# Buffers, loads and places of work moved in a one-layer encoder kernel with attention and a delta-rule recurrence

## The chip, the cores and the metric

The kernel runs on one core of a Trainium2 chip. The metric is the time of one execution in microseconds of device time (us); lower is better. TensorE is the matrix engine (PE in the profile; PEld is its loading of weights), VectorE is DVE, ScalarE is ACT, GpSimd is POOL, and SyncE (SP) issues most transfers. TensorE's clock has two levels, 1.2 and 2.4 GHz; the profile gives the granted clock as a share of 2.4 GHz, so 0.50 is the low level.

## The reference

One layer, on 2048 tokens of width 1024 in float32. The input is normed and projected; half of the columns go to a neighbourhood attention (8 heads of 64, a window of 8 rows by 16 columns on a grid 64 tokens wide), the other half to a gated delta rule that runs over the sequence forwards and backwards (4 heads of 128). Both halves are gated, put side by side, projected out and added to the input.

```python
h = _rmsnorm(x, norm_w)
proj = h @ w_in                                   # 1024 -> 4112 columns
attn = _neighbourhood_attention(aq, ak, av, rpb) * silu(az)
dq, dk, dv = split(silu(conv5(cat([dq, dk, dv]))))          # centred, depthwise
o_f = _gated_delta_chunked(dq, dk, dv, g_f, beta_f)         # S <- decay*S + k^T v_new
o_b = flip(_gated_delta_chunked(flip(dq), flip(dk), flip(dv), flip(g_b), flip(beta_b)))
delta = _rmsnorm(o_f + o_b) * silu(dz)
return x + cat([attn, delta]) @ w_out
```

## The kernel before, in words

A float32 product is made of three products of rounded parts (high by high, high by low, low by high). The work has four stages, one behind the other on TensorE.

The first two stages are the two halves of the projection (`conv_group` for the columns that are convolved, `token_group` for the others; half 1 begins with `conv_group(1, 0)`). Beside them run tasks of a small planner in the code: `tick` moves a clock of the planner's own, `spawn` and each `yield` give a task a due time on it, and a task's instructions are written into the program when its due time has passed. TensorE keeps the program's order there (the class `InOrder` chains each product to the one before). A `token_group` without gates ticks sixteen times 1.42, so 22.72 in all; 24 of its products are 2.84 of the planner's us. The tasks that the change touches are these:

- `turn` transposes a convolved tile of 128 columns, some ticks after its convolution; the tuple `lag` holds how many (half 1 has twelve tiles, `tl` 0 to 11).
- `prepare(half)` solves small triangular systems: `blocks` on VectorE for one direction, then for the other (`ready[d]` is set when a direction's blocks are done, and `solved` with the second). Then joins put the blocks together: `join` issues its loads (E, W and T), yields 14.2, and makes the products `pa`, `pb`, `pc` and `pd`, each 2.84 behind the one before, with a copy on ScalarE between them. In half 0 `both` runs the joins of both directions in step, four times; in half 1 three lanes share ten joins. When the last lane is done it opens the pools for attention's inputs (`open_values`).
- `drain` runs tasks without any projection work beside them.

The third stage is attention (`attend`): 64 units (head pair p, group of rows g, group of columns cg), each with scores on TensorE, a reduction with bias on VectorE, an exponential on ScalarE, a scaling on VectorE, transposes, a copy and the values. The units' instructions are chained to each other on each engine. The recurrence's `step` for both directions is traced behind every seventh unit, the first behind unit 7; its instructions are not chained, and the compiler's scheduler, which lays each engine's order by its own estimate of the times, may put them earlier or later. The four first output weight parts are split (`early_wout`) behind units 52 to 58.

The fourth stage is the output: `late_wout` splits the other four parts of the output weight, and then, for s = 8 to 15, two steps of the recurrence and two `finish` (norm, gate, transposes, the output product `py` and the sum with x).

SBUF is handed out in pools as two stacks, one from either end; a new tile that lies where an old one lay waits until the old one's last use is over. Buffers of attention lie where buffers of the projection lay, and buffers of the output stage lie where attention's lay.

```python
at = {NA_S0 + NA_S1 * i: i for i in range(9)}      # behind units 7, 14, ... 63
...
for s in range(8, 16):
    if s < 15:
        self.step(0, s + 1, False)
        self.step(1, 14 - s, False)
    self.finish(s)
    self.finish(15 - s)
```

Of the kernel before, what the change touches and what calls it, by code (L numbers as in the profile page):

```python
# [70 lines left out]
class Trunk:  # L71
# [198 lines left out]
    def taps(self, half, tl, cb, os):  # L270
# [24 lines left out]
        lag = (21, 29, 36, 33, 30, 27) if half == 0 else (28, 28, 28, 28, 30, 30, 30, 30, 34, 34, 34, 34)  # L295
# [310 lines left out]
    def both(self, pj, c0, c1, sj):  # L606

        W = [pj.tile([128, 8, 128], F32, name=f"wb{d}") for d in range(2)]
        T = [pj.tile([128, 8, 64], F32, name=f"tb{d}") for d in range(2)]
        for t in W + T:  # L610
            self.G.memset(t, 0.0)
        while len(self.ready) < 2:
            yield 1.4
        for c in range(c0, c1, 2):
            e = min(c + 2, c1)
            sinks = [], []
            yield from self.together([self.join(d, c, e, pj, d, W[d], T[d], sinks[d]) for d in range(2)], sinks)
            self.joined += 2
        sj.close()

    def lane(self, i, pj, jobs, sj, c0):

        held = None
        while jobs:
            d = jobs[0][0]
            if d != held:
                W = pj.tile([128, 8, 128], F32, tag=f"wn{i}", name=f"wn{i}{jobs[0][1]}{d}")
                T = pj.tile([128, 8, 64], F32, tag=f"wt{i}", name=f"wt{i}{jobs[0][1]}{d}")
                self.G.memset(W, 0.0)
# [7 lines left out]
            yield from self.together([self.join(d, c, c1, pj, i, W, T, sink)], [sink])  # L637
# [47 lines left out]
    def join(self, d, c, c1, pj, lane, W, T, sink):  # L685
# [13 lines left out]
        yield 14.2  # L699
# [75 lines left out]
    def load_gates(self, p, g):  # L775
        z = self.z[p, g] = self.ns.tile([128, 512], F32, tag="z", name=f"z{p}{g}")
# [8 lines left out]
    def feed(self, p, g):  # L785

        if g == 0:
            if p == 0:
                self.load_bias(0, 1)
                self.load_gates(0, 0)  # L790
            self.load_bias(p, 2)
        elif g == 1 and p < 3:
            self.load_heads(p + 1)
# [28 lines left out]
    def scores(self, p, g, cg):  # L822

        V, A, PE = self.V, self.A, self.PE
        if cg == 0:
            self.feed(p, g)
            mn = self.ns.tile([128, 8], F32, tag="mn", name=f"mn{p}{g}")
            sm = self.ns.tile([128, 8], F32, tag="sm", name=f"sm{p}{g}")
# [55 lines left out]
    def open_recurrence(self, st):  # L884
        P = lambda *a, **k: self.pool(st, *a, **k)
        self.lp, self.op, self.sp, self.rf, self.fx = P("rl", 3), P("ro", 16), P("rs", 2), P("rf", 2), P("rx", 2)
        self.woh, self.wol = [], []
# [13 lines left out]
    def split_wout(self, k, h, l):  # L901
        r = self.fx.tile([128, 1024], F32, tag="x", name=f"wo{k}")
        self.dma(r, self.io["w_out"][:, k])
        self.A.activation(h, r, AF.Copy)
        (self.G, self.V)[k % 2].tensor_tensor(out=l, in0=r, in1=h.bitcast(F32), op=ALU.subtract)
# [3 lines left out]
    def early_wout(self, k):  # L909

        if k < 2:
            t = self.nh[0].tile([128, 2048], F32R, tag="qk"[k], name=f"wo{k}p")
            self.split_wout(k, t[:, :1024], t[:, 1024:])
        else:
            self.split_wout(k, *(self.nv[0].tile([128, 1024], F32R, tag=f"v{2 * k - 4 + i}", name=f"wo{k}p{i}") for i in range(2)))
# [5 lines left out]
    def step(self, d, c, first):  # L921
# [12 lines left out]
        G.tensor_tensor(out=kt, in0=kt, in1=self.eK[:, u0 : u0 + 4].unsqueeze(2).to_broadcast([128, 4, 128]), op=ALU.mult)  # L934
# [3 lines left out]
        for h in range(4):  # L938
            PE.matmul(pk[:, h], kq[:, h, 0], s0[:, h], start=True, stop=True)  # L939
# [38 lines left out]
    def finish(self, c):  # L978
# [16 lines left out]
        na = fp.tile([128, 4, 128], F32, tag="na", name=f"na{c}")  # L995
        dma(na, self.na_d.rearrange("(p k) n -> k p n", k=128)[:, :, cs])
        x = self.fx.tile([128, 1024], F32, tag="x", name=f"x{c}")
        dma(x, self.io["x"][cs])
# [4 lines left out]
        for j, t in enumerate((na, o)):  # L1003
# [7 lines left out]
            V.tensor_tensor(out=lo[:, sl], in0=pt, in1=hi[:, sl].bitcast(F32), op=ALU.subtract)  # L1011
        last = c in (0, 15)
# [17 lines left out]
    def run(self):  # L1030
        with ExitStack() as st:
# [84 lines left out]
            self.late_wout()  # L1116
            for s in range(8, 16):
                if s < 15:
                    self.step(0, s + 1, False)
                    self.step(1, 14 - s, False)  # L1120
                self.finish(s)
# [67 lines left out]
```

## Time and profile before

| what | value |
|---|---|
| time, median of 3 runs | 1439.64 us (1437.33 to 1440.28) |
| the profiled execution: its own time | 1437.78 us |
| the profiled execution: span from first to last instruction | 1436.0 us |
| TensorE busy | 1371.1 us, 95% of the span |
| VectorE, ScalarE, GpSimd busy | 904.1, 664.1, 174.0 us |
| mean granted clock of TensorE | 0.985 |

The span has some 1.8 us around it in the profiled execution's time. The stages stand in the span about like this: half 0 of the projection to 428 us, half 1 to 893, attention to 1166, output to the end. A busy share near 100% of TensorE in a stretch means that TensorE's own work sets the length of that stretch.

### The profile page before, as it was taken

Reading aid. Unit: us, or ns where it says so; the run is one execution under the profiler, and the core shown is the slowest. Engines: PE = TensorE matmul, PEld = TensorE weight load, DVE = VectorE, ACT = ScalarE, POOL = GpSimd, SP = SyncE. Lnnn points to the kernel's source line nnn. Section 1 sums busy time; section 2 is a strip of 40 time slices with the busy share of each in tenths; the row PEclk is TensorE's granted clock in tenths of the full one; section 3 lists DMA queues with packets and bytes.
Section 4 is the critical chain, followed back from the end, with each engine's and each line's share of the span. In section 5 each row is a group of like instructions: output and inputs, shape, how many; then the busy total and the mean of one; then the engine's idle time right before and its main releaser. Section 6 shows DMA issues by size and latency. Waiting matters only on the chain.

```text
span 1436.0 us, 28123 instructions
## 1 busy us (share of the span) xinstructions
PE 1371.1 (95%) x10570; PEld 1181.9 (82%) x10570; DVE 904.1 (63%) x2211; ACT 664.1 (46%) x1630; POOL 174.0 (12%) x206
## 2 busy tenths in 40 slices
PE   7999999999799998999999999899999989999998
PEld 6788988999696886887999888677777767888887
DVE  5689645667434657796887210667768758766773
ACT  6475235733254555464434443656667642221220
POOL 0001102121000021011110110010001012111110
PEclk9999999999899999999999999999999999999999
DMA  9263346774465443678656843999887466765632
GB/s 340 75 237 106 85 132 208 263 218 115 94 197 191 158 133 136 191 240 283 165 126 186 211 135 118 316 313 250 249 224 259 146 186 195 219 199 188 198 103 73
DMA packets 274621, 267.91 MB, mean 187 GB/s; under 512 B 92982, under 2 KB 218038, under 8 KB 273462
## 3 DMA queue, kind: packets, MB, share of 16 engines
q1 hardware_dynamic: 229276, 211.39, 50.0%
q10 hardware_dynamic: 45210, 54.73, 11.2%
q8 instruction: 84, 1.38, 0.4%
q14 instruction: 51, 0.42, 0.1%
HBM read 186.70 MB, written 79.36 MB: 185 GB/s over the span
## 4 chain that ended last, share of the span: by engine, by line
PE 43%; DMA 6%; DVE 3%; ACT 1%; SPq 1%; issue 0%; ACTq 0%; POOL 0%; DVEq 0%; POOLq 0%
PE pt L65 8%; PE py L1021 4%; PE py L1020 4%; PE py L1019 4%; PE po L874 4%; PE sc L839 3%; PE pt L860 3%; PE pz L945 2%; PE pk L939 2%; PE pi L961 2%; PE pS L951 2%; PE pq L959 2%; DMA tab<-in_rpb 1%; DMA kv<-kv_d 1%; DMA e<-ad_d 1%; DMA na<-na_d 1%
## 5 line engine op out<-in xcount | busy, mean ns | idle before, releaser
L65 PE MATMUL pt<-wh_t,xh 128*128 128x256 f32 (+1 forms) x1024 | 297.5, 291 | 0.0
L65 PE MATMUL pt<-wl_t,xh 128*128 128x256 f32 (+1 forms) x1024 | 289.2, 282 | 0.0
L65 PE MATMUL pt<-wh_t,xl 128*128 128x256 f32 (+1 forms) x1024 | 288.8, 282 | 0.0
L65 PEld LDWEIGHTS pt<-wh_t,xh 128*128 128x128 f32 x1024 | 194.0, 189 | 1.9
L65 PEld LDWEIGHTS pt<-wl_t,xh 128*128 128x128 f32 x1024 | 194.2, 190 | 0.4
L65 PEld LDWEIGHTS pt<-wh_t,xl 128*128 128x128 f32 x1024 | 193.9, 189 | 0.0
L65 PE MATMUL pc<-xh,wh_c 128*128 128x512 f32 x384 | 158.1, 412 | 9.6 <-ACT xh L173 8.0
L65 PE MATMUL pc<-xl,wh_c 128*128 128x512 f32 x384 | 153.3, 399 | 1.6 <-DVE xl L174 1.6
L65 PE MATMUL pc<-xh,wl_c 128*128 128x512 f32 x384 | 152.6, 397 | 0.0
L284 DVE SCALAR_TENSOR_TENSOR ca<-cb,cw,ca 128x1022 f32<-128x1022 f32 (+1 forms) x96 | 123.4, 1285 | 2.0
L844 DVE CUSTOM_DVE_ANT_1 s<-sc,tab 128x384 f32<-128x384 f32 (+2 forms) x128 | 67.6, 563 | 81.4 <-PE sc L839 46.7
L845 ACT ACTIVATE s<-s,mn 128x384 f32<-128x384 f32 (+2 forms) x128 | 78.7, 616 | 77.7 <-DVE mn L844 77.7
L65 PEld LDWEIGHTS pc<-xh,wh_c 128*128 128x128 f32 x384 | 73.3, 191 | 27.5 <-ACT xh L173 8.4
L65 PEld LDWEIGHTS pc<-xl,wh_c 128*128 128x128 f32 x384 | 73.1, 190 | 18.5 <-DVE xl L174 3.2
L65 PEld LDWEIGHTS pc<-xh,wl_c 128*128 128x128 f32 x384 | 72.9, 190 | 17.2
L150 DVE TENSOR_TENSOR wl_t<-wr_t,wh_t 128x512 fp32r<-128x512 f32 (+1 forms) x80 | 58.1, 739 | 37.9 <-ACT wh_t L149 37.1
L934 POOL TENSOR_TENSOR kv<-kv,eK 128x512 f32<-128x512 f32 x32 | 33.7, 1053 | 373.0 <-DMA kv<-kv_d 221.7
L384 ACT ACTIVATE tb<-pt,rstd 128x256 f32<-128x256 f32 x64 | 30.4, 475 | 93.8 <-PE pt L65 74.5
L669 DVE TENSOR_TENSOR X<-U 112x30 f32<-112x30 f32 (+29 forms) x120 | 54.0, 450 | 27.5 <-DMA U<-ad_d 13.2
L839 PE MATMUL sc<-k,q 64*128 64x384 f32 (+2 forms) x256 | 64.9, 550 | 5.4 <-DVE mn L844 5.4
L860 PE MATMUL pt<-ident,s 128*128 128x128 f32 (+1 forms) x448 | 66.5, 278 | 1.3 <-ACT pts L862 1.3
L862 ACT ACTIVATE pts<-pt 96x384 f32<-96x384 f32 (+3 forms) x128 | 62.6, 531 | 8.2 <-PE pt L860 8.2
(268 smaller groups left out, 2880.1 us busy)
## 6 DMA issues: line engine op xcount, KB each, us to landing
wr_t<-in_wt SPq DMA_DIRECT2D x64, 256.0 KB
kq<-kq_d SPq DMA_DIRECT2D x32, 512.0 KB
kv<-kv_d SPq DMA_DIRECT2D x32, 512.0 KB
wr_c<-in_wc SPq DMA_DIRECT2D x48, 256.0 KB
xr<-in_xt SPq DMA_DIRECT2D x16, 512.0 KB
xt<-in_xq SPq DMA_DIRECT2D x16, 512.0 KB
pkq<-kq_d SPq DMA_DIRECT2D x16, 512.0 KB
pgb<-gt_d SPq DMA_DIRECT2D x16, 512.0 KB
```

What stands on the lines that cost most here:

```text
L65: self.t.chain("PE", self.e.matmul(*a, **k))
L150: self.V.tensor_tensor(out=l, in0=r, in1=h.bitcast(F32), op=ALU.subtract)
L284: V.scalar_tensor_tensor(ca, in0=cb[:, j : j + n], scalar=self.cw[:, tl, j : j + 1], in1=ca, op0=ALU.mult, op1=ALU.add)
L839: self.chain("PE", PE.matmul(ps[j], self.q[p][own, q0 : q0 + 128], self.k[p][own, r0 : r0 + nr, c0 : c0 + ncl], start=True, stop=True))
L844: self.chain("V", V.tensor_tensor_reduce(out=v3(s), in0=v3(ps[j]), in1=self.tabs[j, NA_TY[g]][:, :, t0 : t0 + ncl], scale=-1.0, scalar=1e3 ...
L845: self.chain("A", A.activation(s, s, AF.Exp, bias=u["mn"][:, a : a + 1], scale=-1.0, accum_out=u["sm"][:, a : a + 1]))
L860: self.chain("PE", self.PE.transpose(pt[:M, b], u["s"][cg, j][:, b * M : b * M + M], self.ident))
L862: self.chain("A", self.A.activation(t[:M, :nb], pt[:M, :nb], AF.Copy))
L874: self.chain("PE", self.PE.matmul(u["po"][own, cg % 2], self.vs[p, cg][:M, b0 + b, own], u["pts"][cg, j][:M, b], start=(b == 0), stop=(b = ...
L1019: PE.matmul(py[n], hi[:, k], self.woh[k][:, ns], start=(k == 0), stop=False)
L1020: PE.matmul(py[n], hi[:, k], self.wol[k][:, ns], start=False, stop=False)
L1021: PE.matmul(py[n], lo[:, k], self.woh[k][:, ns], start=False, stop=(k == 7))
```

## The change

It moves buffers, loads and a few operations; what is computed stays the same.

- `lag` of half 1 has other values (tiles 2 and 3: 30 for 28; 4 to 7: 35 for 30; 10 and 11: 32 and 30 for 34).
- `both` issues the loads of the first join of a direction as soon as that direction is ready, and then waits 26 instead of 14.2 for the products; later joins of half 0 are as they were. In half 1 every join waits 17 instead of 14.2.
- Attention's scores `s`, gates `z` and small sums `mn` and `sm` get a pool of their own, `nsa`, opened in `open_values`; the gates of the first unit and the queries and keys of the second head pair are loaded there too, instead of in `feed`.
- The first products `pk` of the first four chunks that the recurrence meets (two steps of both directions) are chained into attention's order on TensorE, at the place where they are traced.
- In the steps of the output stage (`out=True`) ScalarE scales `kt` in four pieces, where GpSimd did it in one. In all steps that add to `oacc` (`first` is false) VectorE scales `pq` and adds it in one operation per head, where ScalarE scaled it and GpSimd added it.
- All low parts of the output weight are made on VectorE (half of them were on GpSimd). The last two parts of the output weight are loaded in `late_wout`, but split in the first `finish`, behind its transposes, and x of that `finish` is loaded behind them.
- The tile `na` of `finish` comes from a pool `rn` that is opened at the start of attention.

```diff
-        lag = (21, 29, 36, 33, 30, 27) if half == 0 else (28, 28, 28, 28, 30, 30, 30, 30, 34, 34, 34, 34)
+        lag = (21, 29, 36, 33, 30, 27) if half == 0 else (28, 28, 30, 30, 35, 35, 35, 35, 34, 34, 32, 30)
...
-        while len(self.ready) < 2:
-            yield 1.4
...
+            joins = [self.join(d, c, e, pj, d, W[d], T[d], sinks[d]) for d in range(2)]
+            if c == c0:
+                for d in range(2):
+                    while d not in self.ready:
+                        yield 1.4
+                    next(joins[d])
+                yield 26
+            yield from self.together(joins, sinks)
...
-        yield 14.2
+        yield 14.2 if c0 == 0 else 17
...
     def open_values(self):
         self.nv = {0: self.pool(self.sr, "nv0", 1, side="right")}
         self.nh[1] = self.pool(self.sr2, "nh1", 1, side="right")
+        self.nsa = self.pool(self.sr2, "nsa", 2, side="right")
+        self.load_gates(0, 0)
+        self.load_heads(1)
...
-            s = u["s"][cg, j] = self.ns.tile([128, 512], F32, tag="s", bufs=6, name=f"s{p}{g}{cg}{j}")[:, :N]
+            s = u["s"][cg, j] = self.nsa.tile([128, 512], F32, tag="s", bufs=6, name=f"s{p}{g}{cg}{j}")[:, :N]
...
-        (self.G, self.V)[k % 2].tensor_tensor(out=l, in0=r, in1=h.bitcast(F32), op=ALU.subtract)
+        self.V.tensor_tensor(out=l, in0=r, in1=h.bitcast(F32), op=ALU.subtract)
...
     def late_wout(self):
+        rest = []
         for k in range(4, 8):
-            self.split_wout(k, *(self.wo.tile([128, 1024], F32R, name=f"wo{i}{k}") for i in "hl"))
+            h, l = (self.wo.tile([128, 1024], F32R, name=f"wo{i}{k}") for i in "hl")
+            r = self.load_wout(k)
+            if k < 6:
+                self.split_wout(r, h, l)
+            else:
+                rest.append((r, h, l))
+        return lambda: [self.split_wout(*a) for a in rest]
...
+        if out:
+            for h in range(4):
+                A.activation(kt[:, h], kt[:, h], AF.Copy, scale=self.eK[:, u0 + h : u0 + h + 1])
+        else:
+            G.tensor_tensor(out=kt, in0=kt, in1=self.eK[:, u0 : u0 + 4].unsqueeze(2).to_broadcast([128, 4, 128]), op=ALU.mult)
...
-            PE.matmul(pk[:, h], kq[:, h, 0], s0[:, h], start=True, stop=True)
+            mm = PE.matmul(pk[:, h], kq[:, h, 0], s0[:, h], start=True, stop=True)
+            if first and c in (0, 1, 14, 15):
+                self.chain("PE", mm)
...
-            o = self.rf.tile([128, 4, 128], F32, tag="oq", name="oq" + n)
-        for h in range(4):
-            A.activation(o[:, h], pq[:, h], AF.Copy, scale=self.eG[:, u0 + h : u0 + h + 1])
-        if not first:
-            G.tensor_tensor(out=self.oacc[c], in0=self.oacc[c], in1=o, op=ALU.add)
+            o = self.oacc[c]
+            for h in range(4):
+                V.scalar_tensor_tensor(o[:, h], in0=pq[:, h], scalar=self.eG[:, u0 + h : u0 + h + 1], in1=o[:, h], op0=ALU.mult, op1=ALU.add)
...
-        na = fp.tile([128, 4, 128], F32, tag="na", name=f"na{c}")
+        na = self.fn.tile([128, 4, 128], F32, tag="na", name=f"na{c}")
...
+        if rest:
+            rest()
+            x = self.fx.tile([128, 1024], F32, tag="x", name=f"x{c}")
+            dma(x, self.io["x"][cs])
```

## Rows read from the trace of the kernel before

**Rows 1.** The page's first part: busy us (share of span), instructions.

```profile
PE 1371.1 (95%) x10570; PEld 1181.9 (82%) x10570; DVE 904.1 (63%) x2211; ACT 664.1 (46%) x1630; POOL 174.0 (12%) x206
```

**Rows 2.** Stretches: length, busy us (instructions) of PE, PEld, DVE, ACT, POOL, clock, DMA share, GB/s.

```profile
360.00:395.00 35.00, 24.56 (x349) 23.81 (x349) 15.01 (x50) 10.62 (x26) 1.90 (x1) 0.85 0.40 94
382.40:390.40 8.00, 6.29 (x101) 5.96 (x104) 0.00 (x0) 1.59 (x4) 0.00 (x0) 0.60 0.52 153
...
570.00:575.00 5.00, 4.75 (x16) 3.81 (x17) 3.15 (x3) 3.98 (x19) 0.29 (x1) 0.69 0.26 107
795.00:842.00 47.00, 40.77 (x526) 39.20 (x524) 9.29 (x31) 19.37 (x47) 10.01 (x8) 0.96 0.74 178
...
893.00:900.30 7.30, 1.94 (x15) 1.16 (x14) 0.51 (x3) 1.53 (x3) 0.52 (x1) 0.80 0.87 286
...
900.30:946.00 45.70, 41.02 (x307) 30.15 (x308) 28.37 (x99) 26.74 (x73) 4.16 (x4) 0.88 1.05 316
...
1090.00:1106.00 16.00, 13.86 (x126) 10.45 (x124) 14.40 (x41) 11.67 (x30) 5.83 (x3) 1.00 0.76 260
1166.00:1200.00 34.00, 24.88 (x130) 20.63 (x129) 22.45 (x58) 11.16 (x23) 10.49 (x7) 0.80 0.72 211
...
1200.00:1400.00 200.00, 200.00 (x1166) 174.65 (x1165) 140.32 (x427) 45.76 (x105) 28.27 (x24) 1.00 0.59 186
```

**Rows 3.** TensorE in order of time: start, length, work, [idle before, what ended it].

```profile
382.42 0.31 PE L65 MATMUL pa<-tb,e 32*32 32x32 f32 x2 [8.74 <-DMA tb<-ut_d]
...
570.25 0.48 PE L68 MATMUL ptr<-ident,co 128*128 128x128 f32 x1 [4.68 <-ACT to L314]
...
806.14 0.22 PE L65 MATMUL pb<-wn,y 32*32 32x32 f32 x2 [2.87 <-ACT y L708]
...
835.44 0.24 PE L65 MATMUL pb<-wn,y 32*32 32x32 f32 x2 [3.20 <-ACT y L708]
...
900.32 2.92 PE L839 MATMUL sc<-k,q 64*128 64x384 f32 x6 [5.37 <-DVE mn L844]
...
939.39 2.05 PE L939 MATMUL pk<-S,kq 128*128 128x128 f32 x8 [3.25 <-DMA kq<-kq_d]
...
1178.67 0.80 PE L1019 MATMUL py<-wo0p,chi 128*128 128x512 f32 x1 [4.60 <-ACT chi L1010]
...
1192.28 0.48 PE L1009 MATMUL ct<-ident,oacc 128*128 128x128 f32 x1 [3.34 <-DVE oacc L1000]
```

**Rows 4.** The chain that ended last, 885 to 945 and 1164 to 1200.

```profile
893.72 5.81 DMA v_d<-tb
...
900.12 9.48 DMA tab<-in_rpb
909.61 13.08 DMA kv<-kv_d
...
1172.01 11.00 DMA na<-na_d
```

**Rows 5.** VectorE in order of time, 1150 to 1212.

```profile
1187.37 2.29 DVE L50 SCALAR_TENSOR_TENSOR fny<-fnt,fny 128x4 f32<-128x4 f32 x1
...
1191.47 0.16 DVE L50 SCALAR_TENSOR_TENSOR co<-fnt,fny 128x4 f32<-128x4 f32 x1
```

**Rows 6.** GpSimd in order of time, 1150 to 1212.

```profile
1184.78 2.54 POOL L969 TENSOR_TENSOR oacc<-oacc,oq 128x512 f32<-128x512 f32 x2 [12.88 <-ACT oq L967]
```

**Rows 7.** One line's instructions: ns min/median/max, first and last start.

```profile
L905 DVE TENSOR_TENSOR wo1p<-wo,wo1p x1: 1210/1210/1210, 1094.5 to 1094.5; 128x1024 fp32r<-128x1024 f32 x1
```

**Rows 8.** Transfers issued from 890 to 950: count, size of one.

```profile
q<-qk_d SPq DMA_DIRECT2D x1, 1024.0 KB
```

**Rows 9.** Groups by line, 1200 to 1400: busy us, mean ns, idle before.

```profile
L969 POOL TENSOR_TENSOR oacc<-oacc,oq 128x512 f32<-128x512 f32 x13 | 16.9, 1298 | 33.1 <-ACT oq L967 29.6 <-DVE fnt L48 1.7 <-DVE f L942 1.7
L967 ACT ACTIVATE oq<-pq,eG 128x128 f32<-128x128 f32 x52 | 14.9, 369 | 10.1 <-PE pq L959 10.1
...
L942 DVE SCALAR_TENSOR_TENSOR f<-pk,eG,kv 128x128 f32<-128x128 f32 x52 | 14.6, 342 | 2.6 <-PE pk L939 2.2
```

More of the change, by code (lines that the diff above doesn't have):

```diff
@@ L636, in lane @@
             sink = []
-            yield from self.together([self.join(d, c, c1, pj, i, W, T, sink)], [sink])
+            yield from self.together([self.join(d, c, c1, pj, i, W, T, sink, c0)], [sink])
             self.joined += 1
@@ L683, in blocks, with join @@
         self.ready[d] = True
-    def join(self, d, c, c1, pj, lane, W, T, sink):
+    def join(self, d, c, c1, pj, lane, W, T, sink, c0=0):
         dma, A, PE = self.dma, self.A, self.PE
@@ L775, in load_gates @@
     def load_gates(self, p, g):
-        z = self.z[p, g] = self.ns.tile([128, 512], F32, tag="z", name=f"z{p}{g}")
+        z = self.z[p, g] = self.nsa.tile([128, 512], F32, tag="z", name=f"z{p}{g}")
         self.dma(z, self.z_d[p * 128 : p * 128 + 128, g * 512 : g * 512 + 512])
@@ L789, in feed @@
                 self.load_bias(0, 1)
-                self.load_gates(0, 0)
             self.load_bias(p, 2)
         elif g == 1 and p < 3:
-            self.load_heads(p + 1)
+            if p:
+                self.load_heads(p + 1)
             self.load_bias(p + 1, 0)
@@ L826, in scores @@
             self.feed(p, g)
-            mn = self.ns.tile([128, 8], F32, tag="mn", name=f"mn{p}{g}")
-            sm = self.ns.tile([128, 8], F32, tag="sm", name=f"sm{p}{g}")
+            mn = self.nsa.tile([128, 8], F32, tag="mn", name=f"mn{p}{g}")
+            sm = self.nsa.tile([128, 8], F32, tag="sm", name=f"sm{p}{g}")
             om = self.ns.tile([128, 8, 64], F32, tag="om", name=f"na_o{p}{g}")
@@ L886, in open_recurrence @@
         self.lp, self.op, self.sp, self.rf, self.fx = P("rl", 3), P("ro", 16), P("rs", 2), P("rf", 2), P("rx", 2)
+        self.fn = P("rn", 2)
         self.woh, self.wol = [], []
@@ L912, in early_wout, with step @@
             t = self.nh[0].tile([128, 2048], F32R, tag="qk"[k], name=f"wo{k}p")
-            self.split_wout(k, t[:, :1024], t[:, 1024:])
+            self.split_wout(self.load_wout(k), t[:, :1024], t[:, 1024:])
         else:
-            self.split_wout(k, *(self.nv[0].tile([128, 1024], F32R, tag=f"v{2 * k - 4 + i}", name=f"wo{k}p{i}") for i in range(2)))
+            self.split_wout(self.load_wout(k), *(self.nv[0].tile([128, 1024], F32R, tag=f"v{2 * k - 4 + i}", name=f"wo{k}p{i}") for i in range(2)))
     def late_wout(self):
+        rest = []
         for k in range(4, 8):
-            self.split_wout(k, *(self.wo.tile([128, 1024], F32R, name=f"wo{i}{k}") for i in "hl"))
-    def step(self, d, c, first):
+            h, l = (self.wo.tile([128, 1024], F32R, name=f"wo{i}{k}") for i in "hl")
[5 more added lines that the diff above has]
+        return lambda: [self.split_wout(*a) for a in rest]
+    def step(self, d, c, first, out=False):
         V, A, G, PE, dma, lp = self.V, self.A, self.G, self.PE, self.dma, self.lp
@@ L994, in finish @@
         self.from_tiles(dz, self.dz_d, c)
-        na = fp.tile([128, 4, 128], F32, tag="na", name=f"na{c}")
+        na = self.fn.tile([128, 4, 128], F32, tag="na", name=f"na{c}")
         dma(na, self.na_d.rearrange("(p k) n -> k p n", k=128)[:, :, cs])
-        x = self.fx.tile([128, 1024], F32, tag="x", name=f"x{c}")
-        dma(x, self.io["x"][cs])
+        if not rest:
+            x = self.fx.tile([128, 1024], F32, tag="x", name=f"x{c}")
+            dma(x, self.io["x"][cs])
         for h in range(4):
@@ L1011, in finish @@
             V.tensor_tensor(out=lo[:, sl], in0=pt, in1=hi[:, sl].bitcast(F32), op=ALU.subtract)
+        if rest:
+            rest()
+            x = self.fx.tile([128, 1024], F32, tag="x", name=f"x{c}")
+            dma(x, self.io["x"][cs])
         last = c in (0, 15)
```

18 lines of the change are left out of this document (10 added, 8 removed).

## The prediction

> **What bounds the kernel now.** I read the page's busy times first: TensorE is busy 1371.1 of 1436.0 us, the next engine 904.1 [rows 1]. So the span is TensorE's work, its idle time, and what it loses where its clock is at the low level. Then I cut the span into stretches at TensorE's waits [rows 2]: length less PE busy is idle time, and length times (1 less the clock share) bounds what the low clock costs, since work at 1.2 GHz takes twice as long. Last I read TensorE in order of time, where the brackets name what ended each wait [rows 3], and the chain for what stood behind it [rows 4]. Five places are worth something; between them TensorE is full, as in the output stage from 1200 to 1400, with 200.00 of 200.00 busy [rows 2].
>
> - First join of half 0 (360 to 395): 10.44 idle, the largest wait 8.74 for the second direction's inputs [rows 2, 3]. From 382.4 the clock is 0.60 for 8.0 us: up to 3.2 more.
> - Transposes of half 1 (570): 4.68 idle, and 0.31 of 5.0 us, 1.5, by clock.
> - Joins of half 1 (795 to 842): 47.0 less 40.77 is 6.2 idle, in two waits of 2.87 and 3.20 for ScalarE; 0.04 of 47, 1.9, by clock.
> - Attention's start: 5.4 idle from 893, where VectorE's first score waits 5.81 for the last store of the projection's values [rows 4]; 4.7 idle and 0.12 of 45.7, 5.5, by clock up to 946, with the transfer engines full (share 1.05).
> - Attention's end: 34.0 less 24.88 is 9.1 idle, and 0.20 of 34, 6.8, by clock. The two waits are 4.60 for `chi`, which waited for an 11.00 us load of `na`, and 3.34 for `oacc`.
>
> Another 2.1 idle lies in 1090 to 1106. All of it is some 38 us of idle time and up to 19 of clock: nothing in the change can give more than about 57.
>
> **The change, part by part.** I work on the profiled execution, 1437.78 us (span 1436.0 and 1.8 around it), 1.9 below the median of the runs.
>
> *First join of half 0.* Before, both directions poll at most 1.4 behind `solved` and wait 14.2; now the second direction's loads go out at the same point and the products come 26 behind them. So `pa` is written 11.8 planner us later, behind that much more of a `token_group`, whose ticks are TensorE's own pace. The real wait was 10.4, so it fits. TensorE's order there is the program's, so this one is firm: -10.4 and 0 to -3.2 by clock. The first direction's early loads are worth nothing, since only the second's were waited for. Later joins of half 0 slide by the same 11.8 into `conv_group(1, 0)`, whose x loads share the queue with theirs. I take -11 (bounds 0, if the wait moves along, and -13.6).
>
> *Lags.* The wait at 570 is of tile 4's third transposes for a bank that ScalarE had not yet emptied. Tile 4 now comes 5 planner us later, more than 4.68. -4.7 and up to -1.5; I take -5 (0 to -6.2). The other lags move waits of under 2 us.
>
> *Joins of half 1, 17 for 14.2.* Each product comes 2.8 later, about one group of 24 products. The two waits were for ScalarE, not for a load, so the longer wait helps only as far as ScalarE is late by a fixed time: bounds -8.1 and +3 (one more such wait). I take -1.
>
> *The end of the projection.* This edit has a price that no row shows. A join takes 14.2 and four times 2.84, 25.56 by the planner, now 28.36. Lane 0 makes four of the ten. Lanes start 58.8 behind the point where the convolution's pools close, and seven token groups, 159.0, follow that point. Before, the fourth join's last product is due at 58.8 + 4 x 25.56 - 2.84 = 158.2, just inside. Now its first is due at 58.8 + 3 x 28.36 + 17 = 160.9: the whole join falls behind the last projection product, and the pool that holds attention's new buffers opens behind it. Three gaps of 2.84 are 8.5 if nothing covers them, 0 if attention's first scores do. I take +3.
>
> *Attention's start.* The score buffers no longer lie under the projection's stores, so the 5.81 us wait for `v_d` goes, but they lie where the joins' tiles lay, which are now free later. `pk` in its traced place can't stand at the head of TensorE's queue before its inputs are there, which was the 3.25 wait for `kq`; SP's queue holds w, it, kq and kv for each step, and tables behind them. The loads still have to land (share 1.05), and fewer recurrence products fill the first units. All gone would be -15.6; I take half, -8. With the join it is -5 (+9 to -15.6).
>
> *Early weights.* Two subtractions come to VectorE at 1.21 each [rows 7], in a stretch where it is busy 14.40 of 16. GpSimd no longer runs beside it. -1 (+2.4 to -2.1).
>
> *Attention's end.* `na` has a place of its own, so its load can go as soon as `na_d` is written and no longer when attention's buffers are free; the chunk finished first needs a group of rows that is complete some units before the end. Then `chi` and `clo` no longer stand in front of the norm on VectorE. The norm itself is slow there: a four-column operation takes 2.29 us while GpSimd adds and subtracts [rows 5, 6] and 0.16 once GpSimd is quiet; GpSimd has nothing left to do in this stage. The last two weight parts move behind the transposes: their work (two rounded copies, two subtractions of 1.21) is now behind `chi`, and what waits for them is only the second half of `py`, which has the first halves of two chunks in front of it. x is late next, but is needed only at a chunk's end. Bounds 0 and -15.9; I take -9, leaving 6.9 for the next wait (weights or norm).
>
> *Output stage.* TensorE is full there, so operations off it cost nothing while they fit. VectorE gets 13 accumulations of four pieces. Fifty-two pieces of this form, with a product in PSUM, took 14.6 us of VectorE [rows 9], so it goes from 140.3 to 154.9 of 200; ScalarE loses as many pieces (14.9 us) and gets as many for `kt`. 0, with a rival below. One rule of the Trainium skill speaks against moving this read: "VectorE: DVE Perf Modes", section Specifications, places VectorE nearer to SBUF and ScalarE nearer to PSUM. The rows show no such price: 342 ns a piece on VectorE against 369 on ScalarE [rows 9]. By the rule VectorE's total would be above 154.9, and the sum the same while it stays under 200.
>
> Sum: -11 - 5 - 1 - 5 - 1 - 9 = -32, so 1437.8 becomes 1405.8, and on the median's footing 1439.6 - 32 = 1407.6, say 1408.
>
> **The rivals.**
>
> *A, given back at attention's start.* The late join is not covered (+8.5), and `load_heads(1)` goes out in front of the bias tables that unit 4 needs: q and k are 2 MB [rows 8], 6.6 us at 316 GB/s, while all engines of the transfers are full. The start then costs +9 instead of -5: -18, 1422. For it: 9.48 and 13.08 us landings there [rows 4]. Against it: scores are not chained to the projection and may fill the join's gaps. The Trainium skill, "DMA: Bandwidth & Descriptors", section Issuing engines are not separate DMA queues, has all transfers interleave on the same 16 engines, so an earlier load takes its share from the others; the share of 1.05 agrees.
>
> *B, waits that move.* At attention's end the weights' halves take the place of `na`, and at 570 ScalarE is as late for tile 5 as for tile 4: both terms 0, -18, 1422. For it: ScalarE is busy 3.98 of 5.0 us there [rows 2]. Against it: the `na` wait alone is half of the end's idle time.
>
> *C, no effect.* The second direction's inputs arrive 12 us later too, because their loads are laid behind others in SP's queue, and the other terms cancel: 1437 to 1443. Against it: before, those loads went out as soon as VectorE was done.
>
> *D, slower: VectorE's queue in the output stage.* GpSimd's add waited 29.6 us in 13 for its input [rows 9], 2.3 each, harmlessly. VectorE now holds that wait at the head of its queue, with the state's update and the sums with `py` behind it. Its spare time is 200 - 154.9 = 45.1, or 3.5 per step; beyond that the stage grows by 13 us for each us of wait. To undo 32 us it must wait 5.9 per step; at 7 the result is +13, 1453. Against it: ScalarE, which read `pq` before, waited only 10.1 in 52.
>
> **How the numbers follow.** The forecast has 0.58, A 0.15, B 0.10, C 0.05, D 0.12. About 0.2% (2.9 us) is what a measurement of this kernel can tell from no change. Faster: forecast, A and B, 0.83; same 0.05; slower 0.12. The forecast alone runs from 1391 (48 of the 57 us back) to 1420 (20 back). The range goes to 1432 for A and B with their own spread; C, D and what lies below 1391 are left out, some 0.2.
>
> **What would show it.** Right: no wait of over 2 us of TensorE at `pa` of half 0 and at the third transposes of tile 4; `pk` behind unit 7's products; the first `chi` within 5 us of attention's last products; small VectorE operations at 0.16 us throughout the output stage; PE still full from there. Wrong: products of the last join with idle time between them behind the projection; `s` waiting for a store of `w_d`; a wait for `tab` at unit 4; `py` waiting for the last weight parts; VectorE near 200 of 200 in the output stage. The sum would fail most likely at attention's start, where transfers and not engines set the pace.

## The result: slower by 0.7%

The changed kernel takes 1448.97 us (median of 4 runs, 1446.05 to 1450.55) against 1438.92 for the kernel before: a ratio of 1.0072, 95% interval 1.0051 to 1.0093. The forecast was 1408. The profiled execution of the changed kernel took 1446.05 us. This is the first part of its page:

```profile
PE 1382.0 (96%) x10570; PEld 1186.4 (82%) x10570; DVE 897.3 (62%) x2279; ACT 661.1 (46%) x1620; POOL 130.7 (9%) x172
```

The span is 1444.2, so TensorE is idle for 62.2 us, where it was 64.9 before [rows 1]; its busy time is 10.9 us longer with the same 10570 instructions. These are TensorE's waits in order of time (start, length, work, idle before and what ended it):

```profile
538.87 1.15 PE L65 MATMUL pg<-ga,tri 128*128 128x72 f32 x8 [4.24 <-DVE ga L470]
...
797.37 0.58 PE L65 MATMUL pt<-wh_t,xh 128*128 128x256 f32 x1 [5.18 <-ACT sq L385]
...
885.28 2.93 PE L847 MATMUL sc<-k,q 64*128 64x384 f32 x6 [3.14 <-DVE mn L852]
...
916.45 2.07 PE L847 MATMUL sc<-k,q 64*128 64x512 f32 x2 [16.61 <-DVE mn L852]
...
1202.12 1.26 PE L1036 MATMUL ct<-ident,oacc 128*128 128x128 f32 x4 [5.34 <-DVE oacc L1027]
```

The waits for `tb` at 382, for `to` at 570, for `y` in the joins of half 1 and for `kq` at 939 are gone, as forecast [rows 3]. Four others of 3.14 to 5.34 us stand in their place, and a wait of 16.61 us that nothing before had. The stretches that hold it, attention's end and the output stage (columns as in [rows 2]):

```profile
877.00:922.00 45.00, 22.47 (x140) 13.44 (x136) 11.16 (x40) 14.73 (x41) 3.12 (x3) 0.58 0.97 320
1183.00:1210.00 27.00, 20.97 (x111) 17.63 (x110) 17.31 (x55) 8.78 (x15) 0.00 (x0) 0.87 0.74 216
1210.00:1440.00 230.00, 230.00 (x1301) 199.27 (x1300) 144.70 (x516) 46.64 (x100) 0.00 (x0) 1.00 0.54 170
```

In 45 us at attention's start TensorE is idle for 22.5, and its granted clock is 0.58: most of the rest ran at the 1.2 GHz level, behind the long waits. I counted products of one kind in both timelines of TensorE to see where time comes and goes. Attention's first score comes 16.3 us earlier than before (877.2 against 893.5), its 33rd 10.4 later, its last product of the values 17.1 later, and the output products from the 49th on about 8.6 later to the end (a few records are missing, so a count can be off by one or two). So the projection gave about as much as forecast, the first eight units of attention took 26.7 away, the other units 6.7 more, the way from attention into the output stage gave 8.5 back, and the output stage itself changed nothing.

Why the first units lost it stands in SyncE's queue and VectorE's timeline:

```profile
885.20 0.40 SPq L780 DMA_DIRECT2D v<-v_d  x1
885.70 0.32 SPq L739 DMA_DIRECT2D w_d<-wn  x1
886.34 12.91 SPq L780 DMA_DIRECT2D v<-v_d  x15
...
901.78 0.66 SPq L785 DMA_DIRECT2D z<-z_d  x1
902.53 0.38 SPq L769 DMA_DIRECT2D q<-qk_d  x1
903.01 0.42 SPq L771 DMA_DIRECT2D k<-qk_d  x1
903.52 2.87 SPq L791 DMA_DIRECT2D tab<-in_rpb  x4
```

```profile
884.76 0.46 DVE L852 CUSTOM_DVE_ANT_1 s<-sc,tab 128x288 f32<-128x288 f32 x1 [37.14 <-DMA w_d<-wn]
...
915.83 0.56 DVE L852 CUSTOM_DVE_ANT_1 s<-sc,tab 128x384 f32<-128x384 f32 x1 [22.37 <-DMA tab<-in_rpb]
```

Sixteen loads of values are issued first. They are those of the second head pair, which no unit needs for a long time (the first pair's sixteen are issued between 785 and 809). Fifteen of them hold the queue for 12.9 us, 0.86 each. The tables go out behind them and behind z, q and k, and VectorE waits 22.37 us for one, at its ninth reduction, which is unit 4's. Its first reduction had waited for a join's store of `w_d`, and TensorE's 3.14 us stand behind that. Before, the tables went out before these values, at 900.12, and landed 9.48 us later [rows 4].

### The profile page after: what moved, and what is told of

Read it like the earlier page. It is cut to its first block, busy times and chain, and to the rows that moved or that the text cites. A ratio compares the mean times of both kernels' runs of the same rounds, so it can differ in the third digit from the quotient of the medians.

```text
span 1444.2 us, 28125 instructions
## 1 busy us (share of the span) xinstructions
PE 1382.0 (96%) x10570; PEld 1186.4 (82%) x10570; DVE 897.3 (62%) x2279; ACT 661.1 (46%) x1620; POOL 130.7 (9%) x172
## 4 chain that ended last, share of the span: by engine, by line
PE 85%; DMA 6%; DVE 4%; ACT 2%; SPq 1%; issue 1%; ACTq 0%; DVEq 0%
PE pt L65 23%; PE pc L65 16%; PE pz L65 6%; PE py L1050 4%; PE po L882 4%; PE py L1051 4%; PE py L1052 4%; PE sc L847 4%; PE pt L868 3%; PE pz L971 2%; PE pS L977 2%; PE pi L987 2%; PE pk L65 2%; PE pk L963 2%; PE pq L985 2%
## 5 line engine op out<-in xcount | busy, mean ns | idle before, releaser
L847 PE MATMUL sc<-k,q 64*128 64x384 f32 (+2 forms) x256 | 68.4, 564 | 19.8 <-DVE mn L852 19.8
L674 DVE TENSOR_TENSOR X<-U 112x30 f32<-112x30 f32 (+29 forms) x120 | 57.8, 481 | 24.6 <-DMA ut_d<-X 11.3
L868 PEld LDWEIGHTS pt<-ident,s 128*128 128x128 f32 (+1 forms) x448 | 50.4, 137 | 27.1 <-issue 8.0
L882 PE MATMUL po<-pts,v 96*64 96x128 f32 (+1 forms) x896 | 71.5, 286 | 0.0
```

The source lines that it names most:

```text
L674: V.tensor_tensor(out=x, in0=U[:, :, js, m : m + 1].to_broadcast([P, S, nj, ni]), in1=U[:, :, m : m + 1, is_].to_broadcast([P, S, nj, ni]) ...
L847: self.chain("PE", PE.matmul(ps[j], self.q[p][own, q0 : q0 + 128], self.k[p][own, r0 : r0 + nr, c0 : c0 + ncl], start=True, stop=True))
L868: self.chain("PE", self.PE.transpose(pt[:M, b], u["s"][cg, j][:, b * M : b * M + M], self.ident))
L882: self.chain("PE", self.PE.matmul(u["po"][own, cg % 2], self.vs[p, cg][:M, b0 + b, own], u["pts"][cg, j][:M, b], start=(b == 0), stop=(b = ...
```

## The experiments

All are timed beside the kernel before on the same chip, in four sessions (e1 to e4, e5 to e8, e9 to e12, e13 to e15), each on another chip. The kernel before took 1438.28 to 1440.09 us in them, so a difference between two sessions can be off by some 2 us. "Changed" and "before" name the two kernels; the last column is the ratio to before.

| run | what it is | median us | ratio, 95% interval |
|---|---|---|---|
| e1 | changed, joins 14.2 | 1433.60 | 0.9956 (0.9938 to 0.9974) |
| e2 | changed, attention's buffers and loads as before | 1442.50 | 1.0020 (1.0004 to 1.0036) |
| e3 | before, with the 17 | 1440.39 | 1.0009 (0.9983 to 1.0035) |
| e4 | before, with the first join | 1428.40 | 0.9938 (0.9903 to 0.9972) |
| e5 | changed, no chain | 1428.57 | 0.9915 (0.9893 to 0.9936) |
| e6 | e1 and e2 together | 1427.33 | 0.9916 (0.9890 to 0.9943) |
| e7 | e6, no chain | 1419.73 | 0.9862 (0.9840 to 0.9883) |
| e8 | before, with first join and lags | 1420.86 | 0.9867 (0.9847 to 0.9888) |
| e9 | e7 with the pool `nsa` | 1425.11 | 0.9887 (0.9856 to 0.9919) |
| e10 | e9 with the early loads | 1429.01 | 0.9921 (0.9892 to 0.9949) |
| e11 | e9 with the chain | 1428.18 | 0.9913 (0.9888 to 0.9938) |
| e12 | e9, gate tables later | 1423.12 | 0.9876 (0.9847 to 0.9906) |
| e13 | before, with the output edits | 1438.06 | 0.9988 (0.9967 to 1.0009) |
| e14 | before, with the chain | 1442.64 | 1.0025 (1.0004 to 1.0045) |
| e15 | e8, gate tables later | 1420.91 | 0.9876 (0.9846 to 0.9907) |

### Two theories of the 16.6 us: the 17, or the place

**e1.** The changed kernel with:

```diff
-        yield 14.2 if c0 == 0 else 17
+        yield 14.2
```

> The changed kernel with one number put back: every join waits 14.2 as before, so 17 is gone from half 1; all else as changed. Order theory: the 17 makes the fourth join of a lane end behind the projection, so the pools behind it open later, and the transfers of the second head pair's values (16 issues, 12.9 us of SyncE) are laid in front of the bias tables; VectorE then waits 22.4 us for a table and TensorE 16.6. With 14.2 the tables stand first again: no wait of TensorE over 6 us at attention's start, and about 20 us less than the changed kernel's 1449, so 1424 to 1433. Place theory (the score pool and the early q and k in front push the tables into places that come free late): the 16.6 us wait stays, 1445 to 1452.

**e2.** The changed kernel with attention's buffers and loads as before:

```diff
-        self.nsa = self.pool(self.sr2, "nsa", 2, side="right")
-        self.load_gates(0, 0)
-        self.load_heads(1)
...
-            mn = self.nsa.tile([128, 8], F32, tag="mn", name=f"mn{p}{g}")
+            mn = self.ns.tile([128, 8], F32, tag="mn", name=f"mn{p}{g}")
```

> The changed kernel with attention's buffers and loads as before (no pool nsa, gates and second queries and keys loaded in feed again); the 17 stays. Place theory: the wait of 16.6 us for a table goes, 1424 to 1433. Order theory: the values of the second pair still stand in front of the tables, the wait stays within 4 us of 16.6, and the time within 1444 to 1454; the first score may wait some 5 us more for the last store of the first values, as before the change.

**e3.** The kernel before with:

```diff
-        yield 14.2
+        yield 14.2 if c0 == 0 else 17
```

> The kernel before with nothing but the wait of half 1's joins at 17 instead of 14.2. Order theory: attention's start gets a wait for a table of 10 to 17 us and its low clock, so 12 to 25 us slower than before: 1451 to 1464. Place theory: attention's start as before, and only the two 3 us waits of half 1's joins can move: 1434 to 1442.

The 17 does set the order: with it (e2, e3) the sixteen values are issued in front of the tables, with 14.2 (e1) behind them. But only part of the price follows. e1 wins 15.4 us and keeps a wait of 10.64 at the same place; e2 wins 6.5 and keeps waits of 5.69 and 7.18; and e3, where the values stand first too, is no slower than before to within 0.35%. First e1, SyncE's queue and TensorE's wait:

```profile
887.44 2.29 SPq L785 DMA_DIRECT2D z<-z_d  x1
889.78 0.43 SPq L769 DMA_DIRECT2D q<-qk_d  x1
890.31 0.38 SPq L771 DMA_DIRECT2D k<-qk_d  x1
891.02 2.96 SPq L791 DMA_DIRECT2D tab<-in_rpb  x4
```

```profile
903.38 2.07 PE L847 MATMUL sc<-k,q 64*128 64x512 f32 x2 [10.64 <-DVE mn L852]
```

Here 2 MB of q and k stand in front of the tables, with the transfer engines full (share 1.05 from 889 to 903): the first table is needed at 888 and is there at 902.8, 11.7 us after its issue. Then e3, SyncE's queue and TensorE's waits:

```profile
904.63 13.19 SPq L772 DMA_DIRECT2D v<-v_d  x15
...
921.58 0.97 SPq L783 DMA_DIRECT2D tab<-in_rpb  x2
```

```profile
904.75 2.05 PE L939 MATMUL pk<-S0i,kq 128*128 128x128 f32 x8 [5.00 <-DMA kq<-kq_d]
...
929.44 1.28 PE L839 MATMUL sc<-k,q 64*128 64x512 f32 x2 [3.37 <-DVE mn L844]
```

In e3 the tables are issued as late as 921.58, yet TensorE waits only 5.00 and 3.37 us: between the two waits it works on the recurrence. Both theories fell short; neither has this filler in it. The changed kernel and e2 chain the opening `pk` behind unit 7, so there the recurrence cannot fill the gap. That is the theory of e5.

### The first join and the lags alone

**e4.** The kernel before with:

```diff
+            if c == c0:
+                for d in range(2):
+                    while d not in self.ready:
+                        yield 1.4
+                    next(joins[d])
+                yield 26
```

> The kernel before with nothing but the first join of half 0 changed (early loads, then 26). If the term of the sum holds alone, the 8.74 and 1.69 us waits at pa go and nothing takes their place: 10 to 13 us faster, 1426 to 1430. If the wait of 4.24 us at the gate tables of half 1 (538.9 in the changed kernel) comes from this edit, since later joins of half 0 slide into half 1's first convolutions: 5 to 8 us faster, 1431 to 1435, with that wait in the trace.

The two waits at `pa` go, and a new one comes with this edit alone (TensorE, e4):

```profile
536.26 1.11 PE L65 MATMUL pg<-ga,tri 128*128 128x72 f32 x8 [3.49 <-DVE ga L470]
...
562.45 0.33 PE L68 MATMUL ptr<-ident,co 128*128 128x128 f32 x1 [2.97 <-ACT to L314]
```

Counted by the projection's products, its profile is 11.3 us ahead from 519 to 542 and 6.1 at 550. Measured: 9.9 us by the medians, near the first expectation, though the wait is there.

**e8.** e4 with:

```diff
-(28, 28, 28, 28, 30, 30, 30, 30, 34, 34, 34, 34)
+(28, 28, 30, 30, 35, 35, 35, 35, 34, 34, 32, 30)
```

> The kernel before with the first join of half 0 and the lags changed, nothing else. If the lags are worth the -5 of the sum: 1421 to 1426 (1428.4 without them). If the wait at 570 only moves on: 1427 to 1430. Beside the run before this one it prices the edits of the output stage: the sum has -9 and -1 for them; if the time that they win at attention's end was only recurrence work done earlier or later, the two runs are within 3 us of each other.

It takes 7.5 us less than e4 by the medians (of two sessions), and the wait for `to` is gone. With 0.9867 it is one of the fastest kernels of the study.

### The chain

**e5.** The changed kernel with:

```diff
-            mm = PE.matmul(pk[:, h], kq[:, h, 0], s0[:, h], start=True, stop=True)
-            if first and c in (0, 1, 14, 15):
-                self.chain("PE", mm)
+            PE.matmul(pk[:, h], kq[:, h, 0], s0[:, h], start=True, stop=True)
```

> The changed kernel with pk of the first four chunks not chained into attention's order; all else as changed. Filler theory: the late tables stop TensorE for 16.6 us only because the chain keeps the recurrence's products behind unit 7's; unchained, they run in the gap (in the kernel before with 17 alone the tables came 7 us after being issued at 921.6, and TensorE's waits there were 5.0 and 3.4 us): 1433 to 1441, with products of the recurrence between 895 and 916. Tables-only theory: the lost time is set by the tables' landing whatever the chain does: 1446 to 1452.

20.4 us faster than the changed kernel by the medians, with the values in front of the tables as there. TensorE of e5 in the gap (its profiled execution, 1432.21 us, is the slowest of its six):

```profile
888.57 2.05 PE L963 MATMUL pk<-S0i,kq 128*128 128x128 f32 x8 [4.93 <-DMA kq<-kq_d]
891.06 2.08 PE L969 MATMUL pz<-f,w 128*128 128x128 f32 x8 [0.45 <-DVE f L966]
...
909.10 1.16 PE L975 MATMUL pS<-z,kv 128*128 128x128 f32 x8
910.09 1.06 PE L983 MATMUL pq<-S1i,kq 128*128 128x128 f32 x8
911.54 1.16 PE L985 MATMUL pi<-z,it 128*128 128x128 f32 x8 [0.39 <-DVE S L978]
912.54 1.06 PE L963 MATMUL pk<-S,kq 128*128 128x128 f32 x8
920.38 2.07 PE L847 MATMUL sc<-k,q 64*128 64x512 f32 x2 [6.78 <-DVE mn L852]
```

The table comes no sooner, but TensorE does the first step of both directions meanwhile, and the wait is 6.78 for 16.61, behind one of 4.93 for `kq`. The filler theory holds. The time is below its range; e6 and e7 show a second cost of the chain.

**e6.** The edits of e1 and e2 on the changed kernel, so the chain stays:

```diff
-        yield 14.2 if c0 == 0 else 17
+        yield 14.2
...
-        self.nsa = self.pool(self.sr2, "nsa", 2, side="right")
```

> The changed kernel with 14.2 in every join and attention's buffers and loads as before; the chain of pk stays. If the 10.64 us wait that is left with 14.2 alone comes from q and k (2 MB) in front of the tables: it goes, 1420 to 1427. If it comes from the shorter projection (tables meet the projection's last stores sooner) or from the chain: a wait of 6 to 11 us stays, 1429 to 1434.

The table wait is gone (largest wait there 6.04, at the first scores), so the rest of it came with the pool and the early loads, which this run has not; e11 and e1 tell these two apart.

**e7.** e6 with the edit of e5:

```diff
-                self.chain("PE", mm)
```

> The same with pk unchained as well, so that only the first join, the lags, the early weights and the output stage differ from the kernel before. Filler theory: with the tables in time there is little to fill, within 4 us of the run with the chain, 1418 to 1430. If the chain costs of itself, more than 5 us faster than that run.

7.6 us faster than e6, though the tables come in time in both. The idle time is nearly equal (span less busy: 49.9 in e6, 47.3 in e7), the clock too (0.990, 0.988). What differs is TensorE's busy time, 1376.3 against 1370.5. Attention's values products over 946 to 1150, e6:

```profile
L879 PE MATMUL po<-pts,v 96*64 96x128 f32 (+1 forms) x656 | 52.0, 282 | 0.0
```

and e7:

```profile
L879 PE MATMUL po<-pts,v 96*64 96x128 f32 (+1 forms) x694 | 50.8, 283 | 0.0
```

One takes 0.079 us of TensorE in e6 and 0.073 in e7 (busy by count), though the mean of one alone is the same: they overlap less. TensorE in order of time shows why, e6 and then e7:

```profile
987.33 0.87 PE L879 MATMUL po<-pts,v 128*64 128x128 f32 x10
988.13 1.16 PE L974 MATMUL pS<-z,kv 128*128 128x128 f32 x8
989.12 1.06 PE L982 MATMUL pq<-S,kq 128*128 128x128 f32 x8
990.11 0.65 PE L879 MATMUL po<-pts,v 128*64 128x128 f32 x6
990.69 1.13 PE L844 MATMUL sc<-k,q 64*128 64x512 f32 x4
```

```profile
985.73 1.06 PE L972 MATMUL pS<-z,kv 128*128 128x128 f32 x8
986.63 1.06 PE L980 MATMUL pq<-S,kq 128*128 128x128 f32 x8
987.52 0.60 PE L865 MATMUL pt<-ident,s 128*96 128x128 f32 x4
988.05 1.09 PE L879 MATMUL po<-pts,v 128*64 128x128 f32 x16
989.07 1.13 PE L844 MATMUL sc<-k,q 64*128 64x512 f32 x4
```

With the chain the scheduler lays later steps into the middle of a unit's `po`. The four groups take 3.36 us there (987.33 to 990.69); the same 32 products take 0.90, 0.89 and 1.02 in e7, 2.81 together. Over attention `po` is followed by a recurrence product 26 times in e6 (and in the changed kernel) and 8 times in e7 (and before). The Trainium skill, "TensorEngine Tiling (Array Packing)", section Key Properties, says that a change of tiling mode drains TensorE. The rows fit that: `po` is a 128 by 64 tile and the recurrence 128 by 128, the break of one group cost 0.55 us here, and breaks in the middle of `pt` (128 by 128; 29 in e7, 9 in e6) cost nothing that the rows show.

**e14.** The kernel before with nothing but the chain:

```diff
+            if first and c in (0, 1, 14, 15):
+                self.chain("PE", mm)
```

> The kernel before with nothing but the chain of the opening pk. The prediction counted on it (no pk that waits 3.25 us for kq at the head of TensorE's queue): 1434 to 1438. If the chain costs of itself, because products of the recurrence then stand in the middle of attention's groups and because nothing fills TensorE's waits at the start: 3 to 8 us slower, 1442 to 1447, with the busy time of TensorE 2 to 6 us above 1371.1.

2.6 us slower by the medians of that session, 0.25% by the ratio, its interval just above 1; TensorE is busy 1377.6, 6.5 more than in [rows 1]. The `po` row of e14 over 946 to 1150:

```profile
L874 PE MATMUL po<-pts,v 128*64 128x128 f32 (+1 forms) x672 | 52.4, 282 | 0.0
```

0.078 each again, with 23 changes from `po` to the recurrence. The 3.25 us wait for `kq` is gone, as the prediction had it [rows 3]; the chain costs more than it.

### The pool and the early loads

**e9.** e7 with the pool, its loads still in `feed`:

```diff
+        self.nsa = self.pool(self.sr2, "nsa", 2, side="right")
...
-            s = u["s"][cg, j] = self.ns.tile([128, 512], F32, tag="s", bufs=6, name=f"s{p}{g}{cg}{j}")[:, :N]
+            s = u["s"][cg, j] = self.nsa.tile([128, 512], F32, tag="s", bufs=6, name=f"s{p}{g}{cg}{j}")[:, :N]
```

> The run without chain, with 14.2 and with attention's buffers as before (1419.7), plus the pool nsa alone: its loads stay in feed. If the place of the scores is worth what the prediction said, the 5.5 us wait at attention's first scores for the last store of the values goes: 1413 to 1418. If the tables' deeper place takes it back: 1419 to 1424, with a wait for a table.

The wait of 5.48 at the first scores is gone; in its place `pk` waits 6.75 for `kq` at 887.77. The runs spread from 1416.8 to 1429.5, and the intervals of e7 and e9 overlap: the median is above both expectations, and the pool gives nothing that could be measured.

**e10.** e9 with:

```diff
+        self.load_gates(0, 0)
+        self.load_heads(1)
```

> The changed kernel with 14.2 and without the chain, so early gates, queries and keys included. If q and k in front of the tables cost of themselves (the tables landed 11.6 us after their issue with them, 9.5 before): 2 to 8 us slower than the run with the pool alone. If they cost only where the chain leaves TensorE nothing else to do: within 2 us of it. Beside the changed kernel without the chain (1428.6) it prices the 17: 3 to 9 us.

3.9 us over e9, intervals overlapping. Waits do not explain it: TensorE is idle 48.8 us in e10 and 48.4 in e9, but busy 1377.6 against 1366.7. Here the scheduler breaks the groups of `po` without any chain, 23 times for 8 in e9. The `po` row of e10 over 946 to 1150:

```profile
L882 PE MATMUL po<-pts,v 128*64 128x128 f32 (+1 forms) x688 | 54.2, 282 | 0.0
```

That is 0.079 each. So all six kernels with the chain have 23 to 26 such changes, but the chain is not the only way to get them. Against e5, which has the 17 besides, e10 is 0.4 us slower. This doesn't price the 17 without the chain: e5 has 7 such changes, and 6.7 us more idle time.

**e11.** e9 with the chain:

```diff
+                self.chain("PE", mm)
```

> The pool nsa alone, with the chain and 14.2. If the chain costs the same everywhere (7.6 in the pair of runs with attention's buffers as before): 7 to 9 us slower than the same without the chain. If the chain costs by the length of the wait that it leaves uncovered, and the pool leaves none: at most 5 us slower.

3.1 us over e9, overlapping; TensorE busy 1376.6 against 1366.7. Against it e1, which has the early loads besides, is 5.4 us slower: with the chain these loads cost, by the wait of 10.64 where e11 has 4.77.

### The new wait at the gate tables

**e12** is e9, and **e15** is e8, with:

```diff
-            yield 21
+            yield 21 if c0 == 0 else 26
```

> The pool alone without the chain, and half 1's gate tables 5 planner us later (26 for 21 in front of their products), so that the 4.25 us wait that the first join's edit brought goes. If that wait is a lateness of VectorE's chain of small operations: 3 to 6 us faster than without this edit. If the chain on VectorE slides along with the products: within 2 us, and the wait stays.

> The kernel before with the first join of half 0, the lags, and half 1's gate tables 5 planner us later. If the 4.25 us wait at the gate tables' products is worth its length: 1415 to 1418. If what is won there is lost again before the projection's end: 1419 to 1423, as without this edit.

In both the wait is gone, and neither time falls by more than its spread (e12 2.0 us under e9, whose runs spread over 12.6; e15 1420.91, e8 1420.86). e15 has other waits before the projection ends, in the joins of half 1:

```profile
750.38 1.06 PE L65 MATMUL pa<-wt,e 32*32 32x32 f32 x32 [2.11 <-ACT y L713]
...
824.24 0.24 PE L65 MATMUL pb<-wn,y 32*32 32x32 f32 x2 [4.01 <-ACT y L713]
```

where e8 had 2.82 in one. So the wait is a lateness that the joins take back.

### The output stage

**e13.** The kernel before with the edits of the output weights and the output stage alone, of them:

```diff
-        na = fp.tile([128, 4, 128], F32, tag="na", name=f"na{c}")
+        na = self.fn.tile([128, 4, 128], F32, tag="na", name=f"na{c}")
...
+                rest.append((r, h, l))
...
+                V.scalar_tensor_tensor(o[:, h], in0=pq[:, h], scalar=self.eG[:, u0 + h : u0 + h + 1], in1=o[:, h], op0=ALU.mult, op1=ALU.add)
```

> The kernel before with the edits of the output stage and the output weights alone (the pool rn for na, kt on ScalarE, pq added on VectorE, low weight parts on VectorE, the last two split in the first finish). The sum gave them -9 and -1: 1428 to 1431. If their waits only give place to recurrence work laid elsewhere, as the pair 1419.7 and 1420.9 says: 1436 to 1441. If VectorE's queue is a bound: over 1442.

-2.0 us by the medians, no measurable difference; the pair e7 and e8, which these edits (early weights among them) tell apart, says -1.1. Yet at the place itself most of the forecast came true. Stretches of e13:

```profile
1090.00:1166.00 76.00, 73.20 (x634) 56.16 (x632) 56.41 (x180) 50.67 (x137) 4.35 (x4) 0.96 0.55 177
1166.00:1200.00 34.00, 29.55 (x204) 24.89 (x205) 22.88 (x75) 12.28 (x23) 0.00 (x0) 0.95 0.82 240
```

From 1166 to 1200 TensorE is idle 4.5 us where it was 9.1, and the clock is 0.95 for 0.80 [rows 2]: together nearly 10 us. Over the span, however, TensorE is busy 1375.9, 4.8 more than before, at a mean clock of 0.982 for 0.985. Counted by products, as above, e13's first score comes 0.4 us earlier than before, its 193rd 1.3 later, its last 4.9 later, and its last output product 2.1 earlier. So attention's end gives 7.0, but 3.6 of it had been lost just before, where the early weights are made (VectorE, then TensorE):

```profile
1104.52 1.23 DVE L909 TENSOR_TENSOR wo2p<-wo,wo2p 128x1024 fp32r<-128x1024 f32 x1 [2.68 <-ACT wo2p L908]
...
1105.51 1.51 PE L860 MATMUL pt<-ident,s 128*96 128x128 f32 x6 [2.79 <-ACT pts L862]
```

The low part of this weight was GpSimd's. Now VectorE waits for ScalarE's copy of it, and attention's next reduction stands behind; from 1104 to 1114 the granted clock is 0.66, where it was 1.00 before. e7, e9 and e12, which have these edits and no chain, wait 2.47 to 4.01 us there and lose 3.2 to 5.9 between the 193rd score and the last; e4, e8 and e15, without them, at most 0.3. No run has the early weights alone, and the other 1.7 us that e13 loses up to the 193rd score stay open.

## Why the prediction was wrong

**First join: right.** -11 forecast, -9.9 alone (e4, against 1438.28 in its session); the wait at the gate tables came with it, unforeseen, and cost nothing that e15 could find.

**Lags: right.** -5 forecast, -7.5 (e8 less e4), a little beyond the bound of -6.2.

**Joins of half 1: small, as said.** The two waits for `y` went, and a wait of 5.18 for `sq` came. Behind it ScalarE waited 15.54 us at a weight load that stood in SyncE's queue behind a store of a join. At the projection's end the profile of the changed kernel is some 3.5 us ahead of e1's.

**End of the projection: the place was right, the price wrong.** The last join did fall behind the last product. The +3 priced its gaps on TensorE. The cost came through the queue: the pools open later, and the scheduler laid sixteen loads in front of the tables.

**Attention's start: the failed step.** The prediction took -8 there, "fewer recurrence products fill the first units" and the wait for `kq` gone, and gave -5 with the join. In the profile the first eight units lose 26.7 us instead. By the runs, the edits that meet there (chain, pool, early loads and the 17) were forecast at -6 (-8, +3 and -1), and cost 29.2: the changed kernel less e7, which lacks just these. The prediction read the chain as a gain. It is a loss. It takes from TensorE the only work that it has while a table is late: without it the changed kernel is 20.4 us faster (e5). And with the tables in time it still costs 2.6 (e14) to 7.6 us (e6 less e7), where the groups of `po` are broken and TensorE is busy 6.5 and 5.8 us longer. Rival A had the mechanism, q and k in front of the tables, at +9; e1 against e11 gives 5.4 for it. What it lacked were the sixteen loads and the chain, so its 1422 was too low. The prediction had named the place as the likeliest to fail, and two of its signs came true there: `s` waited for a store of `w_d`, and unit 4 for `tab`.

Following the medians from before: first join -9.9 (e4), lags -7.5 (e8), output edits -1.1 (e7), chain +7.6 (e6), pool +0.9 (e11), early loads +5.4 (e1), and the 17 +15.4. Each step is one median less the one before it, so that they add up to the whole is no test of them, and the prices hold in this order. Pool, early loads and the 17, +21.7 of it with the chain, come to +8.8 without it (e5 less e7): they are not additive.

**Early weights: the wrong sign.** -1 forecast, bounded by two subtractions of 1.21 us on a VectorE with time to spare. What it lacked was VectorE's wait for ScalarE's copy; in e13 3.6 us are lost at this place.

**Attention's end: -7 at the place for -9, and little in the sum.** e13 shows it: output edits and early weights together were forecast at -10 and gave -2.0, and -1.1 between e7 and e8. In the changed kernel the first half of rival B came true besides: the last two weight parts take the place of `na`. VectorE there:

```profile
1200.57 1.23 DVE L917 TENSOR_TENSOR wol<-wo,woh 128x1024 fp32r<-128x1024 f32 x1 [7.12 <-ACT woh L916]
1201.71 1.13 DVE L1027 SCALAR_TENSOR_TENSOR oacc<-oacc,co,dz 128x128 f32<-128x128 f32 x4
```

The program has the split behind the transposes; in VectorE's order its first half stands in front of the norm of the next chunk, waits for a weight part that was issued at 1189.35, and TensorE waits 5.34 for `oacc` behind it. e1, e10 and e11 have the same wait at 5.3 to 6.1.

**Output stage: right, and rival D wrong.** TensorE is busy 230.00 of 230 and VectorE 144.70. The new operation came on top of VectorE's work as forecast, yet the total did not grow: before, VectorE was busy 150.91 us from 1200 to 1430. The new operation over 1200 to 1400 waited for nothing:

```profile
L995 DVE SCALAR_TENSOR_TENSOR oacc<-pq,eG,oacc 128x128 f32<-128x128 f32 x48 | 13.4, 341 | 0.0
```

The Trainium skill's rule on VectorE's place ("VectorE: DVE Perf Modes", Specifications) shows no price here: 341 ns a piece, where ScalarE took 369 [rows 9]. The four-column operations of the norm take 0.16 us throughout, 161 ns in the mean, now that GpSimd is quiet; before, those that write `fnt` took 203 and 259 in the mean from 1200 to 1430.

**A sum of the prediction.** The idle times that it lists come to 42.6 us, not 38, so its bound on the whole change was some 61.5 and not 57. The forecast is not made from that bound.

A version that beats both kernels: e8 (two edits) and e7 take 1420.86 and 1419.73, 1.3 to 1.4% under before.

## What to carry to other kernels

An order that is written out for one engine also forbids that engine to fill its waits: before chaining independent work, ask what else the engine can run if the first transfer of the stage is late, and whether the work then lands inside groups of another tile shape. A due time that slips past the end of a stage can reorder a load queue; read the queue's order at the seam, and count issue time in it, not only bytes. Price edits that meet at one place together, since each of these alone cost next to nothing or little.

## What the hardware showed

- Issuing is a cost of its own: fifteen loads of `v` held SyncE for 12.91 us, 0.86 each, where a load of q or k of 1024 KB took about 0.4.
- TensorE's `po` products, 96 or 128 by 64, took 0.073 us each in e7 with 8 changes from them to groups of 128 by 128, and 0.078 to 0.079 in e6, e10 and e14 with 23 to 26.
- Long waits cost twice: around the waits of 3.14 and 16.61 us the granted clock was 0.58 over 45 us; with the wait cut to 6.78 by other work (e5) the stretch had 0.76 over 48. In e13 it was 0.66 over 10 us behind a single wait of 2.79. The stretch of e5:

```profile
879.00:927.00 48.00, 33.31 (x224) 25.06 (x220) 16.72 (x62) 18.30 (x52) 3.12 (x3) 0.76 1.03 317
```
